# Low halves of the down projections' weights: by an adding transfer in place of a subtraction on VectorE

## The chip, the cores and the metric

The kernel runs on one core of one Trainium2 chip. The metric is the device time of one execution in microseconds (us); the time before is the median of three runs. Engines are named as in the profile: PE (TensorE, matmul; PEld is its weight load), DVE (VectorE), ACT (ScalarE), POOL (GpSimd), SP (SyncE, which issues the loads).

## The reference

A decoder trunk of two layers over 256 tokens and a model width of 2048, all in float32. The first layer mixes tokens by a chunked mLSTM, the second by a differential attention, and each ends in a gated feed-forward block, with a residual around both parts. What the change touches is the last line of that block:

```python
D_FF = ((8 * D_MODEL // 3 + 255) // 256) * 256      # 5632
...
def conv_ffn(xn, w_up, conv_w, conv_b, w_down):
    ...
    gate, val = jnp.split(c, 2, axis=-1)
    return (jax.nn.silu(gate) * val) @ w_down
```

`w_down` is 5632 x 2048 per layer, so the down projections of both layers multiply 256 x 5632 by 5632 x 2048.

## The kernel before

Every float32 product is made from three faster ones. A value is cut into a high half `h` (the value rounded to the type `F32R`) and a low half `l` (the value minus `h`), and x·w is computed as xh·wh + xl·wh + xh·wl. Activations are cut once; weights are cut as they stream in. One load on SP's queue brings 1 MB of raw weights into a `raw` tile (four such buffers, shared with the `diff` tiles below). For an "ordinary" granule, which is two k-tiles of 128 rows by 512 columns, `granule` takes a `w2` tile (five such buffers), lets ACT copy the raw weights into its high half and lets DVE write raw minus high into its low half. PE then has 12 products of 128x512 for the granule: for each k-tile and each of the two token halves one with xh and one with xl on the high half, and one with xh on the low half.

Each layer's feed-forward block works in two parts of 22 k-tiles (`half`). After the up projections of a part have filled `hidden`, `gemm_sevenths` does the down projection in groups of 512 output columns, four groups in each part, three in the last part of the second layer, whose last columns are done by `finish`. So there are 15 groups in four stages. In a group the k-tiles 0 to 3, 8 to 11 and 16 to 19 are ordinary, six granules of them. The k-tiles 4 to 7, 12 to 15 and 20, 21 (`MIXED`) go through `sevenths`: a pair of k-tiles is multiplied by 7 block products in place of 8, from raw blocks and from differences of them (`diff`), which DVE makes first; each pair takes two `w2` tiles and 21 products of 128x256, here called mixed products. A mixed tile's halves are made as an ordinary one's, by ACT and DVE.

A tile scheduler sets the order on every engine when the program is built, by its own estimate of durations; on the chip each engine keeps that order and waits by semaphores. An engine that waits holds up everything behind it. A `w2` buffer is refilled when PE's last product with the tile that had it is done; a `raw` buffer is loaded again when its last reader is done.

Of the kernel before, what the change touches and what calls it, by code (L numbers as in the profile page):

```python
# [10 lines left out]
F32 = mybir.dt.float32  # L11
# [3 lines left out]
AF = mybir.ActivationFunctionType  # L15
ALU = mybir.AluOpType
# [20 lines left out]
G = 512  # L37
NG = D // G
RAW = 4
OUT_AT = (8, 10)  # L40
MIXED = (4, 12, 20)
# [27 lines left out]
def trunk(  # L69
# [7 lines left out]
    act, dve, pool, pe = nc.scalar, nc.vector, nc.gpsimd, nc.tensor  # L77
# [9 lines left out]
    def block(dt, name, width=T):  # L87

        b = big.tile([P, 2 * T + 4], dt, tag="block", name=name)
        return b[:, :width], b[:, width:2 * width], b[:, :2 * width]  # L90

    def tmp(name, rows=P, dt=F32):
        return work.tile([rows, T], dt, tag="tmp", name=name, bufs=8)

    def small_ps(name):
        return sm_ps.tile([P, 512], F32, tag="sm", name=name)
# [17 lines left out]
    def later(granules, fn):  # L114
        clock[1] += 1
        heapq.heappush(waiting, (clock[0] + granules, clock[1], fn))

    def tick():
        clock[0] += 1
        while waiting and waiting[0][0] <= clock[0]:  # L120
            heapq.heappop(waiting)[2]()
# [61 lines left out]
    rows = block(F32, "rows")[0][:, :P]  # L183
# [114 lines left out]
    def split(value, name):  # L298
        h, l, hl = block(F32R, name)
        act.activation(h, value, AF.Copy)  # L300
        dve.tensor_tensor(l, value, h.bitcast(F32), op=ALU.subtract)
        return h, l, hl
# [54 lines left out]
                pe.transpose(ps[:, at:at + P], rows[t][:, n * P:(n + 1) * P], ident)  # L357
        return ps

    def granule(w, c0, cw, k0, kn, raws, j, own=True):  # L360

        kc, hc = WCOLS // cw, WCOLS // cw // 2
        at, hc = k0 % kc, min(hc, kn - k0)
        if at == 0:
            raws[j] = wpool.tile([P, kc, cw], F32, tag="raw", name="raw", bufs=RAW)
            n = min(kc, kn - k0)
            loads.append(nc.sync.dma_start(raws[j][:, :n], w[k0 * P:(k0 + n) * P, c0:c0 + cw].rearrange("(k p) n -> p k n", p=P)))
        part = raws[j][:, at:at + hc]
        if not own:
            pairs = [block(F32R, "w2")[:2] for _ in range(hc)]  # L370
            for i, (h, l) in enumerate(pairs):
                act.activation(h, part[:, i], AF.Copy)
                dve.tensor_tensor(l, part[:, i], h.bitcast(F32), op=ALU.subtract)
            return pairs
        w2 = wpool.tile([P, WCOLS // cw // 2, 2, cw], F32R, tag="w2", name="w2", bufs=HL)
        act.activation(w2[:, :hc, 0], part, AF.Copy)  # L376
        dve.tensor_tensor(w2[:, :hc, 1], part, w2[:, :hc, 0].bitcast(F32), op=ALU.subtract)  # L377
        return [(w2[:, i, 0], w2[:, i, 1]) for i in range(hc)]

    def in_order(kn, hc, groups, lead, held=1):  # L380
# [80 lines left out]
            pairs.append(out)  # L461
        return pairs

    def gemm_sevenths(xs, mixed, w, col0, groups, evac, at):


        kn, raws = len(xs), {}
        for g in groups:
            a, b = (acc_ps.tile([P, 2 * T], F32, tag="acc", name="acc") for _ in range(2))
            c = d = None  # L470
            k0 = 0
            while k0 < kn:
                if k0 in at:
                    if c is None:
                        c, d = small_ps("mix"), small_ps("mix")
                    parts = sevenths(w, col0 + g * G, k0, min(2, (kn - k0) // 2))
                    for p, (b1, b2, b3, t1, t3, t2, t4) in enumerate(parts):
                        k = k0 + 2 * p
                        first, end = k == at[0], k0 == at[-1] and p == len(parts) - 1
                        (x0h, x0l, _), (x1h, x1l, _) = xs[k], xs[k + 1]  # L480
                        s1, s2, s3, s4 = mixed[k]
                        lo, hi = slice(0, P), slice(P, T)
                        c0, c1 = slice(0, T), slice(T, 2 * T)
                        ops = (((x0h[:, lo], x0l[:, lo]), b1, c[:, c0], first),
                               ((x1h[:, lo], x1l[:, lo]), b3, a[:, c1], False),
                               (s4, b2, a[:, c0], False),
                               (s1, t1, d[:, c0], first),
                               (s3, t3, d[:, c1], False),
                               (s2, t2, c[:, c1], False),
                               ((x1h[:, hi], x1l[:, hi]), t4, b[:, c1], False))  # L490
                        for (sh, sl), (th, tl), to, start in ops:
                            for o, (u, v) in enumerate(((sh, th), (sl, th), (sh, tl))):
                                pe.matmul(to, u, v, start=start and o == 0, stop=end and o == 2 and to is not a and to is not b, skip_group_check=True)  # L493
                        if p < len(parts) - 1:
                            tick()
                    k0 += 4
                else:
                    for i, (wh, wl) in enumerate(granule(w, col0 + g * G, G, k0, kn, raws, g)):
                        xh, xl, _ = xs[k0 + i]
                        for t, ps in enumerate((a, b)):  # L500
                            s = slice(t * P, (t + 1) * P)
                            for o, (u, v) in enumerate(((xh, wh), (xl, wh), (xh, wl))):
                                pe.matmul(ps, u[:, s], v, start=(k0 + i == 0 and o == 0), stop=(k0 + i == kn - 1 and o == 2), skip_group_check=True)  # L503
                    k0 += 2
                tick()
            evac(g, (a, b), (c, d))
# [74 lines left out]
    def residual(norm):  # L581
        def evac(g, ps, mix=None):
            if mix is not None:
                mixed_in(g, mix)
            for t in range(2):
                rows = stream[:, t, g * G:(g + 1) * G]
                dve.tensor_tensor(rows, ps[t], rows, op=ALU.add)
            if norm is not None:
                norm.add(g)
        return evac  # L590
# [259 lines left out]
    def conv_ffn(layer, norm, evac_down, finish=None):  # L850

        cw = convs[layer]
        later(2, norm.rstd)
        half = FT // 2
        for part in range(2):
            hidden = [None] * half
            conv_of = {}

            def conv(ps, f):
                u = tmp("u")  # L860
                dve.tensor_tensor(u, ps, norm.r, op=ALU.mult)  # L861
                c = tmp("c")
                act.activation(c, u, AF.Identity, bias=cw[:, 3, f:f + 1], scale=cw[:, 2, f:f + 1])  # L863
                dve.scalar_tensor_tensor(c[:, 1:], u[:, :T - 1], cw[:, 1, f:f + 1], c[:, 1:], op0=ALU.mult, op1=ALU.add)
                dve.scalar_tensor_tensor(c[:, 2:], u[:, :T - 2], cw[:, 0, f:f + 1], c[:, 2:], op0=ALU.mult, op1=ALU.add)
                return c

            def evac_gate(j, ps):
                for n in range(2):
                    c = conv(ps[n], part * half + 2 * j + n)  # L870
                    act.activation(c, c, AF.Silu)
                    conv_of[2 * j + n] = c

            mixed = {}

            def evac_val(j, ps):
                pair = []
                for n in range(2):
                    f = 2 * j + n
                    c = conv(ps[n], FT + part * half + f)  # L880
                    dve.tensor_tensor(c, c, conv_of[f], op=ALU.mult)
                    hidden[f] = split(c, f"hid{f}")
                    pair.append(c)
                if 4 * (j // 2) in MIXED:
                    mixed[2 * j] = mix(pair)

            for j in range(half // 2):
                gemm(norm.sets[0], w_up[layer], part * half * P, [j], evac_gate)
                gemm(norm.sets[0], w_up[layer], D_FF + part * half * P, [j], evac_val)
            rows = w_down[layer, part * half * P:(part + 1) * half * P]  # L890
            if part == 0:
                gemm_sevenths(hidden, mixed, rows, 0, range(NG), residual(None), MIXED)
            elif finish is None:
                gemm_sevenths(hidden, mixed, rows, 0, range(NG), evac_down, MIXED)
            else:
                gemm_sevenths(hidden, mixed, rows, 0, range(NG - 1), evac_down, MIXED)
                finish(hidden, rows)


# [273 lines left out]
```

## Time and profile before

| | |
|---|---|
| runs | 2247.50 to 2247.94 us, median 2247.64 of 3 |
| the profiled execution | span 2246.0 us from first to last instruction; no time of its own is listed beside it |
| PE, PEld busy | 2236.4 and 1953.4 us |
| DVE, ACT, POOL busy | 1800.5, 1297.7 and 112.4 us |
| loads | 416.9 MB on SP's queue, 56.7% of the 16 DMA engines' span |

The span is what the chain of waits covers. A busy PE only says that products stood one behind another; how far apart they start is read from the timeline. A product's duration in the trace is longer than the distance to the next one, since products overlap. A share of busy time is a mean over stages, so the down projections are looked at in a window of their own.

### The profile page before, as it was taken

To read this page: it belongs to the slowest core of one execution; us is meant where nothing else is said; L and a number is where in the kernel's file an instruction comes from. 1 tells how busy PE (TensorE), PEld (TensorE's weight loads), DVE (VectorE), ACT (ScalarE), POOL (GpSimd) and SP (SyncE) were. 2 spreads that over 40 slices of the span, in tenths; PEclk is the share of its full clock that TensorE was granted. 3 is DMA by queue.
4 is the path that set the end of the run, shared out by engine and by line. 5 is a ranking of instruction groups with operands and counts; after the bars stand their busy time and mean duration, and the time that the engine had idled before them with its cause. 6 is when DMAs were issued, how large, how long until landed. Compare 5 with 4: busy or idle time off the path is not lost.

```text
span 2246.0 us, 33469 instructions
## 1 busy us (share of the span) xinstructions
PE 2236.4 (100%) x12847; PEld 1953.4 (87%) x12847; DVE 1800.5 (80%) x3007; ACT 1297.7 (58%) x2011; POOL 112.4 (5%) x275
## 2 busy tenths in 40 slices
PE   9999999999999999999999999999999999999998
PEld 9888888888888888888888888888888888888888
DVE  6756868787788877879998985677877988778896
ACT  5455655665554565656655655556565555556554
POOL 0014000000000000000022102300000000000000
PEclk9999999999999999999999999999999999999999
DMA  8554546555545755546566555465555457555464
GB/s 278 177 176 149 186 162 211 192 188 188 187 160 188 234 188 188 190 148 206 193 204 196 161 173 162 154 202 187 188 188 188 159 188 245 190 189 189 145 216 150
DMA packets 325636, 419.04 MB, mean 187 GB/s; under 512 B 9102, under 2 KB 238820, under 8 KB 325476
## 3 DMA queue, kind: packets, MB, share of 16 engines
q1 hardware_dynamic: 325444, 416.89, 56.7%
q8 instruction: 101, 1.65, 0.3%
q14 instruction: 59, 0.48, 0.1%
q10 hardware_dynamic: 32, 0.01, 0.0%
HBM read 414.77 MB, written 2.10 MB: 186 GB/s over the span
## 4 chain that ended last, share of the span: by engine, by line
PE 99%; DVE 0%; ACT 0%; issue 0%; DVEq 0%
PE acc L411 54%; PE acc L503 16%; PE acc L437 14%; PE mix L493 6%; PE acc L493 4%; PE acc L656 2%; PE val_ps L335 1%; PE acc L521 1%; PE turn_ps L231 0%; PE as_ps L987 0%; PE warm_ps L130 0%; PE turn_ps L637 0%; PE hn_ps L357 0%; PE gps L695 0%; PE as_ps L988 0%; PE an_ps L357 0%
## 5 line engine op out<-in xcount | busy, mean ns | idle before, releaser
L377 DVE TENSOR_TENSOR w<-raw,w 128x1024 fp32r<-128x1024 f32 x679 | 826.6, 1222 | 269.6 <-ACT w L376 267.3
L376 ACT ACTIVATE w<-raw 128x1024 fp32r<-128x1024 f32 x679 | 714.0, 1058 | 490.8 <-PE acc L411 322.8
L411 PE MATMUL acc<-x_f,w 128*128 128x512 f32 (+1 forms) x5632 | 987.5, 337 | 0.0
L411 PEld LDWEIGHTS acc<-x_f,w 128*128 128x128 f32 x5632 | 861.5, 188 | 122.8
L503 PE MATMUL acc<-w,hid 128*128 128x512 f32 x1080 | 268.1, 394 | 0.0
L503 PEld LDWEIGHTS acc<-w,hid 128*128 128x128 f32 x1080 | 195.3, 188 | 39.0
L411 PE MATMUL acc<-x_at,w 128*128 128x512 f32 (+1 forms) x1024 | 182.1, 338 | 0.0
L411 PEld LDWEIGHTS acc<-x_at,w 128*128 128x128 f32 x1024 | 156.6, 188 | 21.9 <-issue 0.2
L458 ACT ACTIVATE w<-diff 128x1024 fp32r<-128x1024 f32 x89 | 94.1, 1057 | 113.1 <-DVE diff L451 83.2
L417 ACT ACTIVATE low<-acc 128x256 f32<-128x256 f32 x216 | 78.9, 385 | 130.6 <-PE acc L411 127.7
L459 DVE TENSOR_TENSOR w<-diff,w 128x1024 fp32r<-128x1024 f32 x89 | 108.9, 1223 | 39.5 <-ACT w L458 39.1
L437 PE MATMUL acc<-w,x_a 128*128 128x512 f32 x576 | 138.0, 396 | 0.0
L437 PEld LDWEIGHTS acc<-w,x_a 128*128 128x128 f32 x576 | 106.8, 188 | 24.2
L493 PE MATMUL mix<-w,mix 128*128 128x256 f32 x801 | 119.4, 281 | 0.0
L418 DVE TENSOR_TENSOR acc<-acc,low 128x256 f32<-128x256 f32 x216 | 84.3, 430 | 38.4 <-ACT low L417 38.0
L493 PEld LDWEIGHTS mix<-w,mix 128*128 128x128 f32 x801 | 107.1, 188 | 2.4 <-DVE w L459 0.2
L863 ACT ACTIVATE c<-u,conv 128x256 f32<-128x256 f32 x176 | 98.2, 593 | 5.9 <-DVE u L861 5.6
L458 ACT ACTIVATE w<-raw 128x768 fp32r<-128x768 f32 x89 | 74.7, 840 | 36.7 <-PE acc L503 22.8
L968 POOL TENSOR_TENSOR sw<-sw,sin_t 32x256 f32<-32x256 f32 x32 | 39.1, 1235 | 1076.9 <-DVE sw L967 1026.4
L437 PE MATMUL acc<-w,x_at 128*128 128x512 f32 x384 | 91.4, 395 | 0.0
L459 DVE TENSOR_TENSOR w<-raw,w 128x768 fp32r<-128x768 f32 x89 | 84.9, 953 | 2.5 <-ACT w L458 2.3
L493 PE MATMUL acc<-w,hid 128*128 128x256 f32 x450 | 86.3, 281 | 0.0
(318 smaller groups left out, 2343.8 us busy)
## 6 DMA issues: line engine op xcount, KB each, us to landing
raw<-in_w_up_dram SPq DMA_DIRECT2D x176, 1024.0 KB
raw<-in_w_down_dram SPq DMA_DIRECT2D x79, 1024.0 KB
raw<-in_m_w_in_dram SPq DMA_DIRECT2D x46, 1024.0 KB
raw<-in_w_kv_dram SPq DMA_DIRECT2D x32, 1024.0 KB
raw<-in_m_w_out_dram SPq DMA_DIRECT2D x16, 1024.0 KB
raw<-in_w_q_dram SPq DMA_DIRECT2D x16, 1024.0 KB
raw<-in_w_o_dram SPq DMA_DIRECT2D x16, 1024.0 KB
raw<-in_w_down_dram SPq DMA_DIRECT2D x15, 512.0 KB
```

The lines of the kernel that those rows point to most:

```text
L376: act.activation(w2[:, :hc, 0], part, AF.Copy)
L377: dve.tensor_tensor(w2[:, :hc, 1], part, w2[:, :hc, 0].bitcast(F32), op=ALU.subtract)
L411: pe.matmul(to, a, b, start=(k == 0 and o == 0), stop=(k == kn - 1 and o == len(ops) - 1))
L417: act.activation(low, p[:, T:], AF.Copy)
L418: dve.tensor_tensor(p[:, :T], p[:, :T], low, op=ALU.add)
L437: pe.matmul(ps[t], a[:, s], b, start=(k == 0 and o == 0), stop=(k == kn - 1 and o == 2))
L458: act.activation(w2[:, :m, 0], src, AF.Copy)
L459: dve.tensor_tensor(w2[:, :m, 1], src, w2[:, :m, 0].bitcast(F32), op=ALU.subtract)
L493: pe.matmul(to, u, v, start=start and o == 0, stop=end and o == 2 and to is not a and to is not b, skip_group_check=True)
L503: pe.matmul(ps, u[:, s], v, start=(k0 + i == 0 and o == 0), stop=(k0 + i == kn - 1 and o == 2), skip_group_check=True)
L656: pe.matmul(ps[j], a, b, start=(k == 0 and o == 0 and j % 2 == 0), stop=(k == KD - 1 and o == 2), skip_group_check=True)
L863: act.activation(c, u, AF.Identity, bias=cw[:, 3, f:f + 1], scale=cw[:, 2, f:f + 1])
```

## The change

In the ordinary granules of the down projections, ACT writes the high half as before, then writes minus the high half into the low half, and a transfer issued from POOL adds the raw weights onto it, in SBUF. The subtraction on DVE is left out there. Mixed granules, the last 512 columns and all other projections are as before.

```diff
-    def granule(w, c0, cw, k0, kn, raws, j, own=True):
+    def granule(w, c0, cw, k0, kn, raws, j, own=True, added=False):
...
         act.activation(w2[:, :hc, 0], part, AF.Copy)
-        dve.tensor_tensor(w2[:, :hc, 1], part, w2[:, :hc, 0].bitcast(F32), op=ALU.subtract)
+        if added:
+            low = w2[:, :hc, 1]
+            act.activation(low, w2[:, :hc, 0].bitcast(F32), AF.Copy, scale=-1.0)
+            pool.dma_start(low, part, accum_op=ALU.add)
+        else:
+            dve.tensor_tensor(w2[:, :hc, 1], part, w2[:, :hc, 0].bitcast(F32), op=ALU.subtract)
...
-    def gemm_sevenths(xs, mixed, w, col0, groups, evac, at):
+    def gemm_sevenths(xs, mixed, w, col0, groups, evac, at, added=False):
...
-                    for i, (wh, wl) in enumerate(granule(w, col0 + g * G, G, k0, kn, raws, g)):
+                    for i, (wh, wl) in enumerate(granule(w, col0 + g * G, G, k0, kn, raws, g, added=added)):
...
-                gemm_sevenths(hidden, mixed, rows, 0, range(NG - 1), evac_down, MIXED)
+                gemm_sevenths(hidden, mixed, rows, 0, range(NG - 1), evac_down, MIXED, True)
```

(The other two calls of `gemm_sevenths` in `conv_ffn` get the same `True`; those of the attention and mLSTM projections don't.) Lines move by 5: the ordinary products of L503 are L508 after, the mixed ones of L493 are L498, the high copies stay L376, those of mixed tiles go from L458 to L463, and the new copy and transfer are L379 and L380.

The scheduler also orders the program anew. PE at the k-tiles 8 to 11 of the second column group in the first down projection, before (`w_` names a w2 tile, `hid` a k-tile of the activations: 5012 is k-tile 8, 5222 is k-tile 10; `mix` the mixed operands and sums; in `x4` at 128x512 stand the four products of a k-tile with the high half, in the following `x2` the two with the low half):

```order
L503 MATMUL acc<-w_6673,hid_5012 128x512 x4
L493 MATMUL mix<-w_6709,hid_5432 128x256 x2
L503 MATMUL acc<-w_6673,hid_5012 128x512 x2
L503 MATMUL acc<-w_6673,hid_5022 128x512 x6
L503 MATMUL acc<-w_6688,hid_5222 128x512 x6
```

PE at the same place after:

```order
L498 MATMUL mix<-w_6634,mix 128x256 x9
L498 MATMUL acc<-w_6634,hid_4803 128x256 x3
L508 MATMUL acc<-w_6681,hid_5012 128x512 x4
L498 MATMUL mix<-w_6719,hid_5432 128x256 x3
L498 MATMUL mix<-w_6722,mix 128x256 x4
L508 MATMUL acc<-w_6681,hid_5012 128x512 x2
L508 MATMUL acc<-w_6681,hid_5022 128x512 x6
L508 MATMUL acc<-w_6697,hid_5222 128x512 x4
L498 MATMUL mix<-w_6722,mix 128x256 x5
L498 MATMUL mix<-w_6725,hid_5651 128x256 x3
L508 MATMUL acc<-w_6697,hid_5222 128x512 x2
```

Seven mixed products of the next mixed k-tiles now stand between the high and the low products of k-tile 8, where two stood, and eight before the low ones of k-tile 10.

ACT at this place before, from the high halves of k-tiles 8 to 11 to those of 16 to 19:

```order
L376 ACTIVATE w_6673<-raw 128x2x512
L376 ACTIVATE w_6688<-raw 128x2x512
L458 ACTIVATE w_6709<-raw 128x3x256
L458 ACTIVATE w_6712<-diff 128x4x256
L458 ACTIVATE w_6715<-raw 128x3x256
L458 ACTIVATE w_6718<-diff 128x4x256
L376 ACTIVATE w_6765<-raw 128x2x512
L376 ACTIVATE w_6780<-raw 128x2x512
```

ACT after (L379 is the new negated copy):

```order
L376 ACTIVATE w_6681<-raw 128x2x512
L376 ACTIVATE w_6697<-raw 128x2x512
L379 ACTIVATE w_6681<-w_6681 128x2x512
L463 ACTIVATE w_6719<-raw 128x3x256
L379 ACTIVATE w_6697<-w_6697 128x2x512
L463 ACTIVATE w_6722<-diff 128x4x256
L463 ACTIVATE w_6725<-raw 128x3x256
L463 ACTIVATE w_6728<-diff 128x4x256
L376 ACTIVATE w_6775<-raw 128x2x512
L376 ACTIVATE w_6791<-raw 128x2x512
L463 ACTIVATE w_6813<-raw 128x3x256
L379 ACTIVATE w_6775<-w_6775 128x2x512
```

The negated copy of the first granule (6681, 6775) stands behind the high copy of the second (6697, 6791), and at k-tile 16 behind a mixed tile's copy too.

PE at the k-tiles 16 and 17 of the same group before (hid 5870 is k-tile 16):

```order
L503 MATMUL acc<-w_6765,hid_5870 128x512 x2
L493 MATMUL mix<-w_6718,mix 128x256 x5
L493 MATMUL acc<-w_6718,hid_5661 128x256
L503 MATMUL acc<-w_6765,hid_5870 128x512 x2
L493 MATMUL mix<-w_6801,hid_6290 128x256 x2
L503 MATMUL acc<-w_6765,hid_5870 128x512 x2
```

And after (hid 4154 is k-tile 0 of the next group, whose tile is 6854):

```order
L508 MATMUL acc<-w_6775,hid_5870 128x512 x4
L498 MATMUL mix<-w_6813,hid_6290 128x256 x3
L498 MATMUL mix<-w_6816,mix 128x256 x9
L508 MATMUL acc<-w_6854,hid_4154 128x512 x4
L508 MATMUL acc<-w_6775,hid_5870 128x512 x2
L508 MATMUL acc<-w_6775,hid_5880 128x512 x6
```

Twelve mixed products and four of the next group's first k-tile now stand ahead of the first product with the low half.

More of the change, by code (lines that the diff above doesn't have):

```diff
@@ L891, in conv_ffn @@
             if part == 0:
-                gemm_sevenths(hidden, mixed, rows, 0, range(NG), residual(None), MIXED)
+                gemm_sevenths(hidden, mixed, rows, 0, range(NG), residual(None), MIXED, True)
             elif finish is None:
-                gemm_sevenths(hidden, mixed, rows, 0, range(NG), evac_down, MIXED)
+                gemm_sevenths(hidden, mixed, rows, 0, range(NG), evac_down, MIXED, True)
             else:
-                gemm_sevenths(hidden, mixed, rows, 0, range(NG - 1), evac_down, MIXED)
+                gemm_sevenths(hidden, mixed, rows, 0, range(NG - 1), evac_down, MIXED, True)
                 finish(hidden, rows)
```

## The prediction

> **What bounds the kernel now.** I read the page's totals first, then the chain of waits and PE's list of waits, to see whether PE is ever late.
>
> ```profile
> span 2246.0 us, 33469 instructions
> PE 2236.4 (100%) x12847; PEld 1953.4 (87%) x12847; DVE 1800.5 (80%) x3007; ACT 1297.7 (58%) x2011; POOL 112.4 (5%) x275
> ...
> PE 99%; DVE 0%; ACT 0%; issue 0%; DVEq 0%
> ```
>
> ```profile
> PE warm_ps L130 <- DVE warm L126: 1.1, 1, 1.1
> PE hn_ps L357 <- DVE conv L1066: 0.3, 1, 0.3
> ```
>
> PE is busy in 2236.4 of 2246.0 us, and the whole list of its waits is these two, 1.4 us. So no work taken off DVE can shorten the kernel as long as PE has the same products to do, and it has: the change adds or removes no matmul. What it can do is make PE wait. The down projections must be read as a stage of their own; here is one column group of the first (the windows view: PE, PEld, DVE, ACT and POOL busy, then clock, DMA share and GB/s):
>
> ```profile
> 698.50:727.50 29.00, 29.00 (x178) 25.80 (x178) 26.17 (x34) 15.18 (x17) 0.00 (x0) 1.00 0.56 179
> ```
>
> A group of 512 columns takes 29.0 us, PE never stops, DVE is at 26.17, ACT at 15.18, POOL does nothing, and the 16 DMA engines are 0.56 busy with loads. There are 15 such groups (4, 4, 4 and 3), with six granules of two ordinary k-tiles each.
>
> **What the change removes and adds.** By form, with counts, busy time and mean ns:
>
> ```profile
> L377 DVE TENSOR_TENSOR w<-raw,w 128x1024 fp32r<-128x1024 f32 x678 | 825.9, 1223 | 269.6 <-ACT w L376 267.3
> L376 ACT ACTIVATE w<-raw 128x1024 fp32r<-128x1024 f32 x678 | 713.5, 1059 | 490.8 <-PE acc L411 322.8 <-PE acc L437 62.5 <-PE acc L503 45.9
> ...
> L458 ACT ACTIVATE w<-raw 128x768 fp32r<-128x768 f32 x89 | 74.7, 840 | 36.7 <-PE acc L503 22.8 <-PE acc L493 5.2 <-ACT c L863 2.9
> ...
> L968 POOL TENSOR_TENSOR sw<-sw,sin_t 32x256 f32<-32x256 f32 x32 | 39.1, 1235 | 1076.9 <-DVE sw L967 1026.4 <-PE acc L411 18.8 <-PE acc L437 14.0
> ```
>
> 15 x 6 = 90 subtractions of 1.22 us leave DVE: 110 us of its work, 7.3 a group. Gain: nothing, since PE did not wait for them. 90 copies of about 1.06 us come to ACT: 6.4 a group, 15.2 + 6.4 = 21.6 of 29.0, so ACT does not become the bound; as load it is hidden under PE, and only its place in the chain below counts. 90 transfers are issued by POOL, whose queue is empty in these stages, so nothing of its own is queued behind them.
>
> **The chain that gets longer.** What matters is the time from the moment PE gives a weight buffer back to the moment its refilled low half must be there. Before, at the third group's k-tiles 8 and 9 (timeline):
>
> ```profile
> 704.41 0.19 PEld L493 LDWEIGHTS acc<-w,hid 128*128 128x128 f32 x1
> ...
> 704.88 2.01 ACT L376 ACTIVATE w<-raw 128x1024 fp32r<-128x1024 f32 x2 [0.45 <-ACT w L458]
> ...
> 707.72 1.22 DVE L377 TENSOR_TENSOR w<-raw,w 128x1024 fp32r<-128x1024 f32 x1
> ...
> 708.50 0.31 PEld L503 LDWEIGHTS acc<-w,hid 128*128 128x128 f32 x2
> ...
> 710.38 1.00 PEld L503 LDWEIGHTS acc<-w,hid 128*128 128x128 f32 x5
> ```
>
> PE leaves k-tiles 2 and 3 at 704.41, ACT makes both high halves in 2.01, DVE has the low half ready at 708.94, and PE first wants it at 710.49: 1.5 us to spare. 34 mixed products stand between 704.41 and 708.50, 0.120 us each. The next rows give an ordinary product and a load:
>
> ```profile
> 720.74 0.37 SPq L446 DMA_DIRECT2D raw<-in_w_down_dram  x1
> ...
> 720.90 4.49 PEld L503 LDWEIGHTS acc<-w,hid 128*128 128x128 f32 x20
> ...
> 725.43 0.42 PEld L493 LDWEIGHTS acc<-w,hid 128*128 128x128 f32 x2
> ...
> 726.04 1.23 DVE L449 TENSOR_TENSOR diff<-raw 128x1024 f32<-128x1024 f32 x1 [0.22 <-DMA raw<-in_w_down_dram]
> ```
>
> 20 ordinary products take 4.53 us, 0.2265 each. The 1 MB load issued at 720.74 is what DVE waits for until 726.04: 5.30 us from issue to landing.
>
> After, call X the time from the end of ACT's negated copy to the landed sum. By the changed order (shown with the change), in a group inside a stage:
>
> 1. k-tiles 8, 9. From the buffer's release PE has 35 mixed, 4 ordinary and 7 mixed products before the first low one: 42 x 0.120 + 4 x 0.2265 = 5.95 us. ACT makes both high halves first and only then negates: 2.01 + 1.0 = 3.0. Loss X - 2.95.
> 2. k-tiles 16, 17. PE has 27 mixed, 4 ordinary, 12 mixed and 4 ordinary: 39 x 0.120 + 8 x 0.2265 = 6.5. ACT has two high halves, a 768-wide copy and the negation: 2.01 + 0.84 + 1.0 = 3.85. Loss X - 2.65.
> 3. k-tiles 2, 3. PE has 12 ordinary, 9 mixed, 12 ordinary, 7 mixed: 16 x 0.120 + 24 x 0.2265 = 7.35. ACT has a high half and the negation: 2.0. Loss X - 5.3, if positive.
>
> At k-tiles 10, 11 and 18, 19 the transfer starts some 2 us after the one before it, and PE has the 8 ordinary products left of that granule, 4 of its own and 7 or 8 mixed first (3.6 us): nothing lost there, by the cover of the stall just ahead. k-tiles 0, 1 have the 16 ordinary and 9 mixed products of the group that ends: also nothing.
>
> **How long X is.** No accumulating transfer and no POOL-issued one stands in this trace, so I bound it.
>
> ```profile
> 8.00:10.00 2.00, 2.00 (x17) 1.95 (x17) 1.55 (x4) 1.27 (x3) 0.00 (x0) 1.00 1.04 401
> ```
>
> At their fullest the engines move 401 GB/s, so the 1.05 MB of a load take 2.6 us and the remaining 2.7 of its 5.30 are issue and landing: 0.37 on SP's queue, 2.33 after it. For the transfer the landing is taken alike (2.33). POOL's issue lies between SP's 0.37 and POOL's costliest row, 1.24; I take 1.0, nearer its own engine's row. The 0.5 MB written take 1.3 us if they count like a load's; 2.6 if both operands, the raw weights and the negated halves, go through the engines. I take 2.6, since the sum needs both. Loads keep the engines busy 0.56 of the time; if the two queues share them equally, the transfer runs at half speed in that part: 2.6 / (1 - 0.28) = 3.6. So X = 2.33 + 1.0 + 3.6 = 6.9 us. The ends are 2.33 + 0.37 + 1.3 = 4.0 and, all of it beside loads, 2.33 + 1.24 + 5.2 = 8.8. On the reads the page Collectives: The Full Stack of the Trainium skill, section The bandwidth ceiling: the fold count and why AG ≠ RS ≠ AR, says that a reducing transfer is about half as fast as a copy because it reads two sources, not because of the addition; by it the sum stays as taken, and by plain bytes it would be the low end's. No run here shows it yet.
>
> **The sum.** A group loses (6.9 - 2.95) + (6.9 - 2.65) + (6.9 - 5.3) = 3.95 + 4.25 + 1.6 = 9.8 us, 15 groups 147. The first group of a stage differs a little; I leave that out. Ends: at 4.0, 1.05 + 1.35 = 2.4 a group, 36; at 8.8, 5.85 + 6.15 + 3.5 = 15.5 a group, 232. The raw buffers are another cost: each is now given back when its transfers have landed, not when DVE has subtracted, so SP's loads in that queue start later by several us. I put it at 0, because the same PE stalls (3.95 and 4.25) cover it; without the cover it would be up to 2 us a group, 30. The runs' median, 2247.64, is 1.6 us above the profiled execution's span of 2246.0. So 2246.0 + 1.6 + 147 = 2395 us.
>
> **Rivals.** (a) Short transfers: the add costs no more than a plain copy and falls mostly between loads, X from 4.0 to 5. For it: loads leave 0.44 of the engines free. Against it: two operands. 36 to 66 us: about 2300.
>
> (b) The DMA engines become the bound. A group's loads take 0.56 x 29.0 = 16.2 us of them; six transfers at 2.6 add 15.6, together 31.8, still below the 38.8 that the group then takes. If an adding transfer cost the engines twice that, 5.2, it would be 16.2 + 31.2 = 47.4: 18.4 more than 29.0, 276 in all, 2524 us. It decides from (38.8 - 16.2) / 6 = 3.8 us a transfer on. Nothing in the trace speaks against such a cost, since it has no transfer of this kind.
>
> (c) The clock falls. PE's last products and the clock after them:
>
> ```profile
> 2235.81 1.93 PE L521 MATMUL acc<-w,hid 128*128 128x256 f32 x15
> ```
>
> ```profile
> 2240.00:2241.00 1.00, 0.00 (x0) 0.00 (x0) 0.83 (x2) 0.57 (x1) 0.00 (x0) 1.00 0.00 0
> 2241.00:2242.00 1.00, 0.00 (x0) 0.00 (x0) 0.00 (x0) 0.00 (x0) 0.00 (x0) 0.85 0.94 352
> 2242.00:2243.00 1.00, 0.00 (x0) 0.00 (x0) 0.00 (x0) 0.00 (x0) 0.00 (x0) 0.50 1.03 393
> ```
>
> PE ends at 2237.74 and the granted clock goes to half at about 2241.7, 4.0 us later. My two long pauses are 3.95 and 4.25 us, just at that edge. If each led to half speed for as long again as the pause that caused it, 4 us with 2 us lost, that is 15 x 4 = 60 us: 2455. For it: those three rows. Against it: the products just before and after a pause, so that few pauses are wholly empty for 4 us. TensorE: Matmul & The Clock Gate of the Trainium skill, Part 1, has the same rule with an idle window of about 3.4 us, which does not restart with the work; by it the clock falls in more of these pauses than by the 4.0 of the rows. The trace agrees that it falls, at 4.0.
>
> (d) Not slower: the transfer lands soon enough. It decides at X = 2.65, where the last of the three losses is gone; then DVE's freed 7.3 us a group do nothing for PE and the time is 2248. Against it: the 2.33 us of landing leave 0.3 for issue and moving together. A gain would need products that PE does faster, for which no row speaks.
>
> **How the numbers follow.** Chances: the forecast (X from 5 to 8.8, 66 to 232 us) 0.47, short transfers 0.19, the DMA engines as bound 0.18, the falling clock 0.11, not slower 0.05. The predicted time is the forecast's, 2395. The range goes from 2295, inside the short case, to 2530, past the price of (b); it leaves out the case (d), a quarter of (a), and those of (b) that are dearer still, together about 0.17. Differences under 0.2%, 4.5 us, cannot be told from none. Slower holds all of the first four, 0.95; of (d), 0.03 is no change and 0.02 faster.
>
> **What would show it.** Right: DVE's lines of the subtraction lose 90 of 679; ACT has 90 more copies; PE's waits, 1.4 us before, name the DMA of the low halves with some 150 us, 2 or 3 of them a group, mostly at k-tiles 16, 17 and 8, 9; a group takes about 38.8 us instead of 29.0. Each step is seen by itself: the pause at k-tiles 8, 9 against 3.95, at 16, 17 against 4.25, and X from the end of the negated copy to the product after the wait. Wrong: DMA share near 1.0 in these stages would make it (b), granted clock under 1.0 in them (c); groups of 31 us (a). If PE waits instead for high halves or differences, the raw buffers, put at 0, are the cost.

## The result, and the profile after

The changed kernel takes 2449.53 us (median of four runs, 2445.64 to 2450.08) against 2247.79 for the kernel before: 201.7 us more, a ratio of 1.0893 with a 95% interval of 1.0878 to 1.0909. The profiled execution took 2449.24 us, with a span of 2447.2.

From the page of the kernel after: the span, the busy times, and the two large DMA queues (packets, MB, share of 16 engines):

```profile
span 2447.2 us, 33767 instructions
PE 2311.9 (94%) x12847; PEld 1995.9 (82%) x12847; DVE 1709.4 (70%) x2917; ACT 1379.2 (56%) x2101; POOL 220.5 (9%) x365
...
q1 hardware_dynamic: 325444, 416.89, 52.3%
q0 software_dynamic: 24480, 47.19, 11.0%
```

PE has the same 12847 products. It now stands still for 135.3 us (2447.2 - 2311.9; 9.6 before), and it is busy 75.5 us longer with the same work. DVE is busy 91 us less and ACT 82 more, for 90 instructions each. Queue q0 holds the 90 new transfers: 11.0% of 2447.2 is 269 us of the 16 engines, 2.99 us each.

The ordinary products of the down projections by line (busy, mean ns, idle before them), and the list of waits (us, times, longest):

```profile
L508 PE MATMUL acc<-w,hid 128*128 128x512 f32 x1080 | 323.3, 453 | 88.0 <-DMA w<-raw 88.0
```

```profile
DVE diff L454 <- DMA raw<-in_w_down_dram: 96.1, 33, 4.6
...
PE acc L508 <- DMA w<-raw: 88.0, 30, 7.8
...
PE mix L498 <- DVE w L464: 28.4, 30, 2.6
...
PE mix L498 <- ACT w L463: 6.9, 19, 0.9
```

PE waited 1.4 us in all before; now its whole list comes to 127.7 us, 88.0 of them for the transfers, in 30 waits for 15 groups. The mean ordinary product grew from 394 to 453 ns. DVE's wait for the raw weights of these stages, which was 2.7 us, is 96.1.

Two column groups of the first stage, to be read against the 29.00 before (windows: PE, PEld, DVE, ACT and POOL busy, clock, DMA share, GB/s), and the DMA row of the transfer's line:

```profile
678.00:719.00 41.00, 33.05 (x177) 27.83 (x177) 20.93 (x29) 21.19 (x23) 7.20 (x6) 0.92 0.86 217
719.00:761.00 42.00, 34.20 (x177) 28.93 (x177) 21.18 (x29) 21.07 (x23) 7.20 (x6) 0.90 0.85 215
```

```profile
DMA to landing us min/median/max: 5.0/8.2/12.8
```

A group takes 41 us instead of 29. Of the 12 more, about 8 are PE standing still (41 - 33.05) and 4 are PE busy for longer with the same products (33.05 - 29.0). Some 2.3 of these 4 are a lowered clock: the first 20 products of the group take 7.04 us (first row of the timeline below), where 19 distances of 0.2265 and a last product of 0.39 make 4.70. The rest lies around the waits, where a product overlaps with no other. Over the whole run, the trace has PE at work for 112 us at half clock, so some 56 of the 75.5 us are the clock's, by this estimate. The DMA engines are at 0.86, up from 0.56. A transfer lands 8.2 us after POOL starts to issue it (median), 5.0 at best.

One group in the timeline, PE's waits for the transfers and the negated copies that each goes back to (two views, one of PE and one of all engines):

```profile
678.71 7.04 PE L508 MATMUL acc<-w,hid 128*128 128x512 f32 x20 [4.68 <-DMA w<-raw]
...
691.09 2.13 PE L508 MATMUL acc<-w,hid 128*128 128x512 f32 x8 [0.66 <-DMA w<-raw]
...
699.99 0.39 PE L498 MATMUL mix<-w,hid 128*128 128x256 f32 x1 [1.50 <-DVE w L464]
...
701.66 3.06 PE L508 MATMUL acc<-w,hid 128*128 128x512 f32 x12 [0.65 <-DMA w<-raw]
...
719.65 7.05 PE L508 MATMUL acc<-w,hid 128*128 128x512 f32 x20 [4.26 <-DMA w<-raw]
```

```profile
682.52 1.06 ACT L376 ACTIVATE w<-raw 128x1024 fp32r<-128x1024 f32 x1 [8.38 <-PE acc L508]
683.61 1.06 ACT L379 ACTIVATE w<-w 128x1024 fp32r<-128x1024 f32 x1
...
695.22 1.04 ACT L379 ACTIVATE w<-w 128x1024 fp32r<-128x1024 f32 x1
...
710.25 1.04 ACT L379 ACTIVATE w<-w 128x1024 fp32r<-128x1024 f32 x1
```

These are k-tiles 16 of one group (678.71), then 2, 8 and 16 of the next. The negated copies end at 684.67, 696.26 and 711.29; the low products start 6.42, 5.40 and 8.36 us later. The three hang on one another: the products behind each landing free the buffer (ACT's copy at 682.52 waits for PE), which is copied, negated and transferred for the next one.

The clock at the pause before 719.65:

```profile
716.00:717.00 1.00, 0.00 (x0) 0.00 (x0) 0.00 (x0) 0.00 (x0) 0.73 (x1) 1.00 1.12 287
717.00:718.00 1.00, 0.00 (x0) 0.00 (x0) 0.82 (x1) 0.00 (x0) 0.00 (x0) 0.76 1.16 213
718.00:719.00 1.00, 0.00 (x0) 0.00 (x0) 1.00 (x4) 0.00 (x0) 0.00 (x0) 0.50 1.12 205
...
724.00:725.00 1.00, 1.00 (x5) 0.78 (x4) 0.00 (x0) 0.97 (x2) 0.00 (x0) 0.82 0.99 348
```

PE's pause began at 715.39 (719.65 less 4.26). The mean of 0.76 puts the fall at 717.5, that of 0.82 the rise at 724.4: half speed for 6.8 us, 4.7 of them while PE worked on the products behind the wait.

### The profile page after: what moved, and what is told of

Same layout as the page of the kernel before. It is cut to its first block, busy times and chain, and to the rows that moved or that the text cites. A ratio compares the mean times of both kernels' runs of the same rounds, so it can differ in the third digit from the quotient of the medians.

```text
span 2447.2 us, 33767 instructions
## 1 busy us (share of the span) xinstructions
PE 2311.9 (94%) x12847; PEld 1995.9 (82%) x12847; DVE 1709.4 (70%) x2917; ACT 1379.2 (56%) x2101; POOL 220.5 (9%) x365
## 3 DMA queue, kind: packets, MB, share of 16 engines
q0 software_dynamic: 24480, 47.19, 11.0%
## 4 chain that ended last, share of the span: by engine, by line
PE 56%; DMA 8%; issue 3%; DVE 1%; ACT 0%; POOLq 0%; DVEq 0%; SPq 0%
PE acc L416 37%; PE acc L508 9%; DMA w<-raw 8%; PE acc L442 6%; PE mix L498 1%; DMA raw<-in_w_down_dram 1%; PE acc L526 1%; PE acc L498 1%; PE val_ps L335 0%; PE turn_ps L231 0%; PE as_ps L992 0%; DVE diff L454 0%; PE as_ps L993 0%; PE an_ps L357 0%; ACT w L376 0%
## 5 line engine op out<-in xcount | busy, mean ns | idle before, releaser
L376 ACT ACTIVATE w<-raw 128x1024 fp32r<-128x1024 f32 x679 | 713.7, 1057 | 641.0 <-PE acc L416 328.9
L382 DVE TENSOR_TENSOR w<-raw,w 128x1024 fp32r<-128x1024 f32 x589 | 717.0, 1221 | 280.1 <-ACT w L376 277.4
L508 PE MATMUL acc<-w,hid 128*128 128x512 f32 x1080 | 323.3, 453 | 88.0 <-DMA w<-raw 88.0
L508 PEld LDWEIGHTS acc<-w,hid 128*128 128x128 f32 x1080 | 231.0, 223 | 147.6 <-DMA w<-raw 97.5
L380 POOL DMA_DIRECT2D w<-raw x90 | 108.2, 1202 | 1740.6 <-PE acc L416 1213.6
L463 ACT ACTIVATE w<-diff 128x1024 fp32r<-128x1024 f32 x89 | 93.6, 1052 | 109.4 <-PE acc L508 86.8
L498 PE MATMUL mix<-w,mix 128*128 128x256 f32 x801 | 123.3, 289 | 14.2 <-DVE w L464 7.8
L498 PEld LDWEIGHTS mix<-w,mix 128*128 128x128 f32 x801 | 107.7, 192 | 23.5 <-DVE w L464 10.8
L454 DVE TENSOR_TENSOR diff<-raw 128x1024 f32<-128x1024 f32 (+1 forms) x52 | 55.6, 1069 | 101.4 <-DMA raw<-in_w_down_dram 96.1
L379 ACT ACTIVATE w<-w 128x1024 fp32r<-128x1024 f32 x90 | 94.4, 1049 | 0.8
```

Of the source, the lines that this page charges most:

```text
L379: act.activation(low, w2[:, :hc, 0].bitcast(F32), AF.Copy, scale=-1.0)
L380: pool.dma_start(low, part, accum_op=ALU.add)
L463: act.activation(w2[:, :m, 0], src, AF.Copy)
```

## The experiments

The first theory was the prediction's: PE waits for low halves that come too late, and the lowered clock (75 us of longer products) comes on top. Rivals: (A) ACT's copies and the new order; (B) the transfers' time on the DMA engines, whoever waits; (C) raw buffers held until a transfer has landed.

### No transfer, half of one, and a copy in place of the add

No transfer:

```diff
-            pool.dma_start(low, part, accum_op=ALU.add)
+            dve.tensor_tensor(low, part, low.bitcast(F32), op=ALU.add)
```

> ACT writes minus the high half as in the changed kernel, but DVE adds the raw weights onto it; there is no transfer. Theory (the loss is PE waiting 126 us for transfers that a chain longer than the depth of the weight buffers brings too late, and 75 us of products at a lowered clock behind these pauses): without a transfer the low half comes only one copy of 1.06 us later than before, and PE had 1.5 us to spare there: 2248 to 2265 us, PE's waits under 15 us, granted clock 1.00. Rival A (ACT's 90 added copies and the order that comes with them are the cost): 2350 us or more. Rivals B (the time that the transfers take from the 16 DMA engines) and C (raw buffers held until the transfers have landed) expect what the theory does here.

2260.76 us, 13.0 over the kernel before (ratio 1.0058, 1.0043 to 1.0073). PE waits 3.5 us for these low halves:

```profile
PE acc L508 <- DVE w L380: 3.5, 8, 1.0
```

Rival A is out as the main cause: the copies, with the order that this program got, are worth 13 us, and the other 189 come with the transfer. The scheduler ordered this program anew, so the changed kernel's own order is not tested alone here.

Half a transfer:

```diff
-            pool.dma_start(low, part, accum_op=ALU.add)
+            pool.dma_start(low[:, :1], part[:, :1], accum_op=ALU.add)
+            dve.tensor_tensor(low[:, 1:], part[:, 1:], low[:, 1:].bitcast(F32), op=ALU.add)
```

> The transfer adds only the first of the two k-tiles (256 KB in place of 512); DVE adds the second. Theory: a transfer now takes some 3.0 us of the engines (11.0% of 2447 us for 90), some 4 us beside loads; half of that is 2.1 us less for each of three waits in a group, 95 us in 15 groups, and pauses of about 2 us no longer bring the clock down, 75 us: about 2280 us, 2265 to 2320, clock 0.99 to 1.00. Rival B, in proportion to the engine time: 2350. Rival C, buffers held nearly as long because landing and issue stay: 2350 to 2400.

2321.91 us (1.0331, 1.0315 to 1.0346), just above the theory's interval and below the rivals'. Queue q0 takes 6.1% of 2319.5 us, 1.57 us a transfer, and a transfer lands 4.1 us after its issue in place of 8.2.

A copy in place of the add, which leaves the order of PE's and ACT's work as in the changed kernel:

```diff
-            pool.dma_start(low, part, accum_op=ALU.add)
+            pool.dma_start(low.bitcast(F32), part)
```

> The transfer copies the raw weights over the negated halves and does not add (the low halves are then the raw weights). Same bytes, same issue, same order and waits. If the price of the transfer is that both operands go through the engines, its engine time falls from 3.0 to about 1.5 us and the time goes to 2265 to 2330, like half a transfer. If the price is the bytes written, the descriptors or the landing, engine time and kernel time stay: 2430 to 2455 us.

2364.45 us (1.0526, 1.0509 to 1.0543): between the two expectations. Its page and the row of its line:

```profile
q0 software_dynamic: 12960, 47.19, 5.2%
```

```profile
L380 POOL DMA_DIRECT2D w<-raw x90: 722/722/911, 631.9 to 2322.1; - x90
...
DMA to landing us min/median/max: 3.1/4.9/9.3
```

5.2% of 2369.8 is 1.37 us of the engines for the same bytes, against 2.99 with the add, and 12960 packets against 24480. POOL's issue is 0.72 in place of 1.20 us and the landing 4.9 in place of 8.2. Adding instead of copying costs 85 us (2449.5 - 2364.5); a plain copy in its place would still have lost 117.

### Which buffer is late

The raw buffer set free early:

```diff
-            pool.dma_start(low, part, accum_op=ALU.add)
+            pool.dma_start(low.bitcast(F32), w2[:, :hc, 0].bitcast(F32), accum_op=ALU.add)
```

> The transfer adds the high half onto minus the high half (the low halves come out as zero), so it does not read the raw buffer, which is free as soon as ACT has copied it. Issue, bytes and PE's wait for the low half stay. Theory (weight buffers): PE's waits for the low halves stay near 90 us and the clock falls as before, DVE's waits for raw loads (96 us) go: 2400 to 2450 us. Rival C (raw buffers are what is late): under 2330 us. Rival B: no change, 2450.

2484.02 us (1.1055, 1.1036 to 1.1073): outside all three expectations, 34 us above the changed kernel. DVE's waits for raw weights went as the theory said; PE's for the transfers were 88.0 us and grew:

```profile
PE acc L508 <- DMA w<-w: 102.6, 40, 5.8
...
DVE diff L454 <- DMA raw<-in_w_down_dram: 17.4, 11, 2.8
```

So taking away the 96 us of DVE's waits won nothing by itself. Why the kernel became slower still is not settled: the scheduler ordered this program anew as well.

No product waits for the transfer:

```diff
-            low = w2[:, :hc, 1]
-            act.activation(low, w2[:, :hc, 0].bitcast(F32), AF.Copy, scale=-1.0)
-            pool.dma_start(low, part, accum_op=ALU.add)
+            high = w2[:, :hc, 0].bitcast(F32)
+            dve.tensor_tensor(w2[:, :hc, 1], part, high, op=ALU.subtract)
+            pool.dma_start(part, high, accum_op=ALU.add)
```

> DVE subtracts as in the kernel before, and POOL's transfer then adds the high half onto the raw weights, which nobody reads any more: 90 adding transfers of 512 KB that hold a raw buffer and fill the DMA engines, but no product waits for one. Theory (PE's wait for the low half, and the clock behind it): 2250 to 2320 us, granted clock 0.99 or more; what is left over 2248 is the price of late raw loads alone. Rival B (engine time, 3.0 us a transfer, whoever waits): 2400 us or more. Rival C (raw buffers held): 2350 or more, with DVE's waits for raw loads near the 96 us of the changed kernel.

2386.61 us (1.0620, 1.0604 to 1.0636). Here the theory failed: 139 us are lost though no product waits for a transfer. Rival C's expectation came in, with 93.9 us of DVE's waits for raw weights; rival B's 2400 was missed by 13. One window of 40 us, SP's queue, PE's largest wait and ACT's waits for the transfer:

```profile
670.00:710.00 40.00, 35.26 (x185) 29.87 (x185) 27.40 (x33) 15.95 (x18) 7.34 (x7) 0.89 0.93 230
```

```profile
SPq L451 <- DMA raw<-w: 339.1, 30, 15.0
```

```profile
PE mix L498 <- ACT w L463: 40.4, 22, 4.9
```

```profile
ACT w L376 <- DMA raw<-w: 24.3, 24, 3.0
...
ACT w L463 <- DMA raw<-w: 17.3, 9, 5.0
```

The loads of mixed tiles wait 339 us for transfers to give their raw buffers back (in the changed kernel the two load lines waited 172.4 and 133.2 us for transfers), the DMA engines are at 0.93, and PE waits for the mixed tiles that are made from those loads. But the run is no test of the raw buffers alone: its transfer reads the high half, so a weight buffer too is refilled only when the transfer has landed, and ACT waits 41.6 us for that. What the two runs show is that the transfer closes two loops, one through the weight buffers and one through the raw buffers, that the first alone, with the raw buffers free, is long enough to stretch the groups (236 us), and that 139 us are lost even when no product reads what the transfer writes. How much the raw buffers would cost by themselves stays open, and no price here may be subtracted from 201.7 to get another. The second theory is that the pace of a group is set by the transfers and loads, through whichever loop is longer, and that what matters is a transfer's time.

Only k-tiles 0 to 3:

```diff
-granule(w, col0 + g * G, G, k0, kn, raws, g, added=added)
+granule(w, col0 + g * G, G, k0, kn, raws, g, added=added and k0 in (0, 2))
```

> Only the granules of k-tiles 0 to 3 use the transfer, 30 in place of 90; the others are as before. The prediction's terms: k-tiles 0, 1 cost nothing, 2, 3 cost X - 5.3 = 1.6 us a group, 24 us: 2272 us. Theory, by the 0.66 us that PE waited there: 2250 to 2275 us, clock 1.00. If every transfer costs alike, a third of 201 us: 2315.

2285.40 us (1.0169, 1.0152 to 1.0186): 37.6 us. The theory's 2250 to 2275, the prediction's 24 us and the third of 201.7 all missed. PE's and DVE's waits:

```profile
DVE diff L454 <- DMA raw<-in_w_down_dram: 37.8, 22, 3.0
...
PE acc L508 <- DMA w<-raw: 18.2, 8, 6.3
```

PE waits for 8 of the 30 transfers only, but for up to 6.3 us, far longer than the 0.66 that the theory took over from the changed kernel; this program's order is its own.

### The fixed part

```diff
-            pool.dma_start(low, part, accum_op=ALU.add)
+            pool.dma_start(low[:, :1, :64], part[:, :1, :64], accum_op=ALU.add)
+            dve.tensor_tensor(low[:, :1, 64:], part[:, :1, 64:], low[:, :1, 64:].bitcast(F32), op=ALU.add)
+            dve.tensor_tensor(low[:, 1:], part[:, 1:], low[:, 1:].bitcast(F32), op=ALU.add)
```

> The transfer adds only the first 64 columns of the first of the two k-tiles (32 KB in place of 512); DVE adds all the rest. What stays is POOL's issue of 1.2 us, the landing and the raw buffer that is held until then; the engine time goes (from 3.0 us to some 0.2). If engine time and the traffic beside the loads are most of the loss: the copy's 13 us without any transfer, and 15 groups x 1 to 2 us for a chain of some 3.5 us: 2270 to 2290 us. If the fixed latency is most of it: 2320 us or more, as with half a transfer (2322).

2298.79 us (1.0228, 1.0213 to 1.0243), nearer the first expectation but above it. Even 32 KB land only after 2.9 us (median), and take 1.5% of 2299.4 us, 0.38 us of the engines each:

```profile
DMA to landing us min/median/max: 2.1/2.9/6.9
```

With the other three, this makes a ladder of ever longer transfers. Only the last two rows have the same order of PE's and ACT's work; the scheduler ordered the others anew, so what their steps are put down to is argued and not shown one by one:

| kernel | us | step |
|---|---|---|
| before | 2247.8 | |
| negated copy, DVE adds | 2260.8 | 13.0: ACT's copy, an order of its own |
| and 32 KB added by transfer | 2298.8 | 38.0: issue, landing, raw buffer held, an order of its own |
| 512 KB copied by transfer | 2364.5 | 65.7: 1.37 us of engine time in place of 0.38 |
| 512 KB added by transfer | 2449.5 | 85.1: 2.99 us in place of 1.37, POOL's issue 1.20 in place of 0.72 |

### The order of the products

The low products of two neighbouring granules behind all their high ones (loops cut to what differs):

```diff
-for o, (u, v) in enumerate(((xh, wh), (xl, wh), (xh, wl))):   # per k-tile and token half
+for low in (0, 1):                                            # over both granules: 16 high, then 8 low
+    for o, (u, v) in enumerate(((xh, wl),) if low else ((xh, wh), (xl, wh))):
```

> The transfers stay as in the changed kernel; in the down projections the products are written in another order: the 16 with the high halves of two neighbouring granules first, then the 8 with their low halves. That puts 12 more products of 0.2265 us, 2.7 us, between the first high and the first low product of k-tiles 8 and 16. Theory: the pauses of 4.3 us at k-tile 16 shrink to about 1.6, too short to bring the clock down: PE's waits from 126 to 60 to 100 us, its slow products from 75 to under 20, 2310 to 2370 us, clock 0.99. Rival B (the DMA engines' time sets the pace): no order of products helps, 2430 us or more.

2393.04 us (1.0645, 1.0629 to 1.0661): 56 us are won back, which puts it between the theory's 2310 to 2370 and rival B's 2430. The waits:

```profile
DVE diff L454 <- DMA raw<-in_w_down_dram: 100.0, 37, 7.7
...
PE acc L524 <- DMA w<-raw: 79.7, 54, 3.9
```

The longest wait fell from 7.8 to 3.9, but there are 54 of them. The same order with half a transfer, and with the copy (this diff together with those of the two shown above):

> Half a transfer (the first k-tile; DVE adds the second) and the products with the low halves written behind the 16 high ones, as in the run with the later lows. If PE's wait is a matter of the chain's length against the work that stands ahead of the first low product, 2.7 us more of that work cover the pauses of about 1.3 us that half a transfer left (49.8 us in 39): 2255 to 2285 us, PE's waits for transfers under 15 us. If the DMA engines' time or the raw loads (59 us of DVE's waits with half a transfer) set the pace, it stays at 2305 to 2325 us.

> A copy in place of the add (the low halves are then the raw weights), full size, and the later lows. The add with later lows took 2393 us, the copy in the changed order 2364. If the second operand's engine time is a loss of its own beside the chain's length, both gains add up: 2364 - 2447 + 2393, about 2310 us (2290 to 2325). If they are two ways of covering the same pause, it takes 2330 to 2365 us.

Half a transfer: 2311.89 us (1.0285, 1.0269 to 1.0302), only 10 less than in the changed order; the expectation of 2255 to 2285 missed, and its rival's 2305 to 2325, with the DMA engines or the raw loads as the pace, held (DVE waits 66.3 us for them, 59.1 in the changed order). The copy: 2313.88 us (1.0295, 1.0277 to 1.0312), as the sum of both gains said (2310). A shorter transfer and a later need for it help by separate amounts while the transfer is what is late; with half a transfer PE's order matters little (10 us), and the loads being late next is the likely reason: PE still waits 29.9 us for transfers there, where under 15 had been expected.

### The clock

Work of no effect in place of the pause: 16 products with a zero block of the identity, ahead of k-tile 16.

```diff
+                        if added and k0 in (16,) and i == 0:
+                            for _ in range(8):
+                                for ps in (a, b):
+                                    pe.matmul(ps[:64], ident_r[64:, :64], wh[64:], start=False, stop=False, skip_group_check=True)
```

> The changed kernel, with 16 products of 512 columns that add zero to the sums put ahead of k-tile 16 in every group, 16 x 0.2265 = 3.6 us of work in place of most of the pause of 4.3 us there; nothing else is touched. If the 75 us of longer products come from the clock that falls in this pause, they go in part and the kernel is faster with more work: 2390 to 2425 us, clock 0.98 or more. If the products are slow for another reason (SBUF or the DMA traffic), the time stays at 2445 to 2460 us.

2447.15 us (1.0881, 1.0865 to 1.0897): unchanged, with 240 products more, as the second expectation said. Its reason (SBUF or DMA traffic) is not shown by that, since the clock did fall. The pause at k-tile 16 was down to 2.28 us, from 717.24 to 719.52, and the clock fell at 719.9, by the mean of 0.98 (0.50 in 720 to 722; it did not fall in the next group's pauses of 1.3 and 1.7 us before k-tiles 8, the last two rows):

```profile
716.00:718.00 2.00, 1.24 (x7) 0.71 (x5) 0.94 (x1) 0.38 (x1) 0.00 (x0) 1.00 1.13 220
718.00:720.00 2.00, 0.48 (x2) 0.44 (x3) 2.00 (x6) 0.00 (x0) 0.00 (x0) 0.98 1.12 205
720.00:722.00 2.00, 2.00 (x7) 1.54 (x6) 1.97 (x4) 0.00 (x0) 0.00 (x0) 0.50 1.13 207
722.00:724.00 2.00, 2.00 (x8) 1.59 (x7) 0.14 (x1) 0.98 (x1) 0.00 (x0) 0.67 1.12 199
738.00:740.00 2.00, 0.75 (x5) 0.66 (x5) 1.69 (x3) 1.58 (x2) 0.93 (x1) 1.00 1.10 220
740.00:742.00 2.00, 0.28 (x4) 0.08 (x2) 1.61 (x2) 0.22 (x1) 0.00 (x0) 1.00 1.09 189
```

So a second filling, with 26 products there and 12 ahead of k-tile 8:

```diff
+                        for _ in range({8: 6, 16: 13}.get(k0 + i, 0) if added else 0):
+                            for ps in (a, b):
+                                pe.matmul(ps[:64], ident_r[64:, :64], wh[64:], start=False, stop=False, skip_group_check=True)
```

> The changed kernel with 26 products that add zero ahead of k-tile 16 (5.9 us) and 12 ahead of k-tile 8 (2.7 us) in every group, as much as PE stood still there. With 16 of them at k-tile 16 alone the pause shrank to 2.3 us and the clock still fell in it, for 3.3 us. If products at half clock right behind the landing delay the next buffer's release and so the next transfer, a clock that stays at 1.00 shortens a group of 41 us by 1.5 to 2.5 us: 2405 to 2430 us. If the transfers and loads alone set the pace: 2440 to 2455 us with the clock at 0.99 to 1.00.

2435.64 us (1.0836, 1.0820 to 1.0853). Two groups, the filling products, DVE's wait, and PE at the k-tiles 16 with which each of the two windows begins:

```profile
678.00:719.00 41.00, 39.78 (x222) 31.40 (x221) 20.54 (x27) 21.42 (x23) 7.20 (x6) 1.00 0.86 214
719.00:760.00 41.00, 38.45 (x212) 30.27 (x212) 20.87 (x27) 21.42 (x23) 7.20 (x6) 1.00 0.88 223
```

```profile
L507 PE MATMUL acc<-w,ident_r 64*64 64x512 f32 x570 | 136.7, 390 | 0.0
```

```profile
DVE diff L454 <- DMA raw<-in_w_down_dram: 202.6, 40, 10.6
```

```profile
679.19 5.93 PE L511 MATMUL acc<-w,hid 128*128 128x512 f32 x24
...
721.95 4.92 PE L511 MATMUL acc<-w,hid 128*128 128x512 f32 x20 [1.23 <-DMA w<-raw]
```

The clock is 1.00, PE has 570 products more, and a group still takes 41 us. Without the filling PE is busy 2393.2 - 136.7 = 2256.5 us, 55 less than after, and the time fell by 14. The result lies between both expectations.

It does not give the price of the clock. The filling takes 136.7 / 15 = 9.1 us a group, which with the 29.0 of the group's own products makes 38.1 of the 41: PE itself is nearly the bound in this kernel, and at the first of the two k-tiles 16 it did not wait for the transfer at all. So 14 us are what the full clock won in spite of the filling, and its worth without filling may be more. The first filling says a little in addition: PE still waited for the landing behind it, the granted clock rose from 0.970 to 0.981, and the time fell by only 2.4 us. There the landing, and not the pace of the products, came last. Whether transfers and loads would hold a group at 41 us with a full clock and no filling is not shown.

## Why the prediction was right, and where it was short

The direction and the main mechanism hold. DVE's relief was worth nothing. DVE lost 90 subtractions and ACT got 90 copies, which were hidden up to the 13 us of the run without a transfer. PE waits for the DMA of the low halves, mostly at k-tiles 16.

**X** was right on average only: 6.42, 5.40 and 8.36 us at k-tiles 2, 8 and 16 of the group shown, a mean of 6.7 against 6.9. The prediction took one X for all three places, but it was too long for k-tiles 2 and 8 and too short for 16. Its parts: 1.20 us of issue, where I took 1.0; 2.99 us of the engines, where I took 2.6 because both operands would count. The landing was taken too long: the quickest transfer landed 5.0 us after its issue began, and 5.0 less 1.20 and 2.99 leaves 0.8, if the three follow one another, where I took 2.33. The run with the copy bears out the choice of 2.6 over 1.3: 1.37 us without the add. The Trainium skill, Collectives: The Full Stack, section The bandwidth ceiling: the fold count and why AG ≠ RS ≠ AR, has the reduce step of a ring at about half a copy's speed, since the add reads two sources; the trace agrees for this transfer within one core, 2.99 against 1.37 us.

**The places.** At k-tiles 16 the pause is 4.26 to 4.68 us, against 4.25. That it agrees so well is luck: X was 8.36 there and not 6.9, but PE also stopped only 4.10 us after the end of the negated copy (711.29 to 715.39) and not 2.65, partly because it waited 0.31 and 0.52 us for mixed tiles before. There X is longest of the three, since the transfers of k-tiles 16, 18 and the next group's 0 are issued within 4 us, and the DMA share is 1.12 to 1.16 in the three microseconds from 716 to 719. At k-tiles 8 the loss is 2.15 (1.50 for a mixed tile behind late raw weights, 0.65 for the transfer) against 3.95, at k-tiles 2 it is 0.66 against 1.6, and in the other 14 groups PE does not wait there at all. So the waits of this group come to 7.9 us with two small ones for mixed tiles, less than the 9.8 of the sum.

**The term that failed** is what the sum left out: a group lost 12, not 9.8, and 15 groups times 12 are 180. The sum counted pauses only and left the pace of the products as it was. PE was busy 4 us longer in the group shown, some 2.3 of them at half clock, which I had as rival (c) and not beside the forecast. My ground against it was that few pauses are empty for 4 us. They need not be: the clock fell 2.1 us into one pause, and in the filled kernel 0.4 us after the end of one of 2.28. Rival (c) was the forecast's 147 us of pauses with 60 of slowed products on top, 2455 us; measured, PE stood still for 126 us more and was busy for 75 more, some 56 of these the clock's. So by the trace the time lies nearer rival (c) than the forecast. What a full clock would have saved is another question: the filled pauses show 14 us at least, and no run shows more.

**The first group of each stage**, left out, accounts for some 16 of the last 22 us: by the starts of the groups these four lost 15.5, 14.7, 16.0 and 18.2 us, 64 in place of 4 x 12. Such a group waits as long at k-tiles 8 as others at 16:

```profile
657.86 5.34 PE L508 MATMUL acc<-w,hid 128*128 128x512 f32 x12 [3.88 <-DMA w<-raw]
```

In the four stages that wait was 3.88, 3.99, 3.89 and 4.26 us, against 0.2 to 1.7 later, about 3 more each; and the first group of the last stage has the one of 7.8 at k-tiles 16, 3 more again.

**The raw buffers, put at 0,** were not free. PE's waits for mixed tiles come to 35 us (28.4 and 6.9), which the prediction had named as the sign. The 1.50 us at 699.99 can be followed back: the low product of k-tiles 2 started at 691.09, when the transfer had landed, and a raw load is issued then; DVE waits for it until 696.39 and makes the differences of that mixed tile late.

```profile
691.18 0.37 SPq L451 DMA_DIRECT2D raw<-in_w_down_dram  x1
...
696.39 1.23 DVE L454 TENSOR_TENSOR diff<-raw 128x1024 f32<-128x1024 f32 x1 [4.60 <-DMA raw<-in_w_down_dram]
```

So the cover by the other pauses, which the prediction counted on, was not complete. That freeing the raw buffers saved nothing all the same is measured, in a program with an order of its own; their price alone stays open.

**Rival (b)** asked for 3.8 us of the engines a transfer; 2.99 came, and 0.86 as DMA share. As a bound over the whole group it is out. Within a group it is half true: around the landings at k-tiles 16 the engines are full, and 85 of the 201.7 us go to the engine time and issue that an add needs beyond a copy. Rivals (a) and (d) fell with X: even the 32 KB transfer, landing after 2.9 us, cost 38.

## What to carry to other kernels

Moving an operation from an engine that was not late to a DMA lengthens a chain, and the test is that chain against the work standing between a buffer's release and its next use; with 32 KB in place of 512, a transfer still cost 38 us here. A transfer that reads a loaded buffer also closes a loop through that buffer, and cutting one loop need not help: here a transfer without the raw buffers held, and one that no product read, both stayed far above the time before. A sum of waits and slowed products tells where time lies, not what it would be worth to remove; putting useless work into the pauses is a quick way to ask, but the work takes time of its own, so the answer is a lower bound.

## What the runs showed of the hardware

- An adding transfer of 512 KB within SBUF took 2.99 us of the 16 engines, 24480 packets for 90 and 1.20 us of POOL each; a copying one 1.37, 12960 and 0.72. An add of 32 KB still took 0.38 us and 0.86 of POOL.
- While adding transfers run beside loads, the DMA share passes 1.1 at 205 to 213 GB/s (717 to 719 above), where loads alone showed 1.04 at 401.
- The clock fell at 717.5, 2.1 us after PE's last product, for 6.8 us, and in the filled kernel at about 720.0, for 3.4; the two short pauses in 738 to 742 left it at 1.00. The prediction's 4.0 us was one case. TensorE: Matmul & The Clock Gate of the Trainium skill, Part 1, says that the clock is judged over a free-running window of about 3.4 us. The lengths of 6.8 and 3.4 fit two windows and one. A window of 3.4 us that ended with the fall at 717.5 would have begun at 714.1, and PE was at work until 715.39, so by this trace a window need not be wholly idle.
